# Decay rows of the SSD scan at 128 contraction rows, y products in another order, down weights in 8 KB runs

## The chip, the cores and the metric

One NeuronCore of one Trainium2 chip runs the whole kernel. The metric is the device time in microseconds (us) of one execution. Three executions of the kernel before are shown; their median is what a change is held against. A second, profiled execution gives every duration below.

## The reference, cut to what matters

A decoder block over 512 tokens of width 1024: RMSNorm with adaptive shift and scale, a Mamba-2 SSD branch beside a pooling branch, an output projection, then a mixture of 32 experts of which each token takes 4, and a final norm. The change touches two places. In the SSD branch, for each chunk of 128 tokens and each head:

```python
a_cum = jnp.cumsum(a, axis=-1)
seg = a_cum[..., :, None] - a_cum[..., None, :]
decay = jnp.exp(jnp.where(causal, seg, -jnp.inf))
CB = jnp.einsum('bclgn,bcsgn->bcgls', Cc, Bc)
y_diag = jnp.einsum('bcgls,bcgels,bcsgep->bclgep', CB, decay, X)
...
y_off = jnp.einsum('bclgn,bcgepn,bcgel->bclgep', Cc, prev, jnp.exp(a_cum))
return (y_diag + y_off).reshape(b, s, SSD_HEADS, P)
```

There are 4 chunks, 4 groups, 8 heads of width 64 in a group. In the experts, for the tokens that chose expert e:

```python
gu = xblk @ w_gu[e] + b_gu[e]
...
return act @ w_down[e] + b_down[e]
```

## The kernel before, in words

All work is written in one program for five engines. TensorE (PE) multiplies, VectorE (DVE) and ScalarE (ACT) work elementwise, GpSimd (POOL) and SyncE (SP) mostly issue transfers. A scheduler in the framework decides, before the run, in which order each engine takes its instructions; on the chip each engine then follows its own list strictly and waits on semaphores.

**Projections.** A product of float32 exactness is made of three products of rounded operands: every loaded weight piece is split into a rounded part and a rest (ACT line 117, DVE line 118), and PE multiplies high by high, high by low and low by high. In `proj` these are lines 265, 266 and 267; in `ssd_out` lines 653 to 655; in the experts lines 1118 to 1120. Each is one matmul of 128 contraction rows, 128 output rows and 512 columns. The experts that got few tokens (the "half" ones) skip the split and multiply float32 directly (line 1113).

**SSD.** The program calls `ssd(g)` for the groups g = 0 to 3, with the projections of group g + 1 written behind it (`proj_bc`, `proj_z`, `proj_xs`), then `ssd_out(g)`. The scheduler interleaves these, so that PE takes projection matmuls while ACT and DVE prepare operands. Group 3 is interleaved with gate projections. In `ssd(g)`, four head pairs `hp` follow one another. For each head of a pair:

- the decay row: a matmul copies the head's row of the cumulated decay `AH` to all partitions (line 601). `AH` is a tile of 64 rows, high parts in rows 0 to 31 and rests in rows 32 to 63, and `E` picks the head;
- ACT forms 4 pieces of the decay (line 604), `exp` of 384 columns for the chunk states (line 606) and `exp` of 512 columns for the inner part (line 607);
- DVE multiplies the two results by the `CB` and `C` products (helper at line 114): `dec` and `eC`.

Then the y products of the pair: 8 matmuls of `Xd` with `dec` (line 617) and 6 of the chunk states `Hs` with `eC` (line 619; the first chunk has no state). Each gives 64 output rows and 128 columns; the head h2 of the pair writes rows 0 to 63 or 64 to 127 of the bank `py`. A float32 matmul stands in the trace as two instructions, so a pair of heads has 28.

```python
for c in range(NB):
    cc = slice(c * P, (c + 1) * P)
    hs = [slice(hp * P + h2 * 64, hp * P + h2 * 64 + 64) for h2 in range(2)]
    for h2 in range(2):
        TE.matmul(py[h2 * 64:(h2 + 1) * 64, cc], c3(Xd)[:, c, hs[h2]], decs[h2][:, cc], start=True, stop=c == 0)
    for h2 in range(2 if c else 0):
        TE.matmul(py[h2 * 64:(h2 + 1) * 64, cc], Hs[c][:, hs[h2]], eCs[h2][:, (c - 1) * P:c * P], start=False, stop=True)
```

So a pair needs three shapes of the PE array: 64 rows by 128 columns (line 601), 128 by 64 (lines 617 and 619) and 128 by 128 (everything else around it).

**Experts.** `fetch` (line 771) loads 1 MB pieces from SP's queue into a ring of buffers: 8 pieces of `wgu` and 4 of `wdn` for each of the 32 experts. A `wgu` piece is 128 rows of 8 KB, one for each partition. A `wdn` piece is 256 rows of 4 KB, two for each partition, which lie 128 rows apart in memory.

Of the kernel before, what the change touches and what calls it, by code (L numbers as in the profile page):

```python
# [10 lines left out]
F32R = mybir.dt.float32r  # L11
BF16 = mybir.dt.bfloat16
I32 = mybir.dt.int32
U32 = mybir.dt.uint32
AF = mybir.ActivationFunctionType
# [5 lines left out]
P = 128  # L21
D = 1024
T = 512
NB = 4
KD = 8
NH = 32
NE = 32
# [41 lines left out]
def hybrid_block(ctx: ExitStack, tc: tile.TileContext, cst, cols, rows, xt, xf, wad0, wada, bada,  # L69
                 wx, wz, wdt, wu, wg, wso, wpl, wpo, wo, wr, ball, wgu, wdn, out):  # L70
    nc = tc.nc
    V, S, G, TE, SP = nc.vector, nc.scalar, nc.gpsimd, nc.tensor, nc.sync
# [9 lines left out]
    def T_(tag, cols_, dt=F32, parts=P):  # L82
        if tag in shared:
            o = shared[tag]
            return Z[0:parts, o:o + cols_]
        uid[0] += 1
        return sb.tile([parts, cols_], dt, tag=tag, name=f"{tag}_{uid[0]}")
# [104 lines left out]
    E = T_("E", 32, F32R)  # L192
# [131 lines left out]

    dt, negA, a2 = T_("dt", P), T_("negA", NH), T_("a2", 2 * P)
    ac, dte, eac, cdk = T_("ac", P), T_("dte", P), T_("eac", P), T_("cdk", P)
    AH = T_("q7", 512, F32R, parts=64)

    def make_dt():
        w = load(wdt, n=256)  # L330
        ps = bank("mm")
        for k in range(KD):
            j = k % 4 * 32
            TE.matmul(ps[j:j + 32, :], w[:, k * NH:(k + 1) * NH], xk(k), start=k < 4, stop=k >= 4)
        dfm = T_("q8", 512)
        S.activation(dfm, ps, AF.Copy)
        pdt = bank("ss")
        for b in range(NB):
            TE.transpose(pdt[:, b * P:(b + 1) * P], dfm[:, b * P:(b + 1) * P], ident)

        dx, da, dq, dp = T_("q9", P), T_("q10", P), T_("q11", P), T_("t1", P)
        V.tensor_reduce(v3(dx), pdt.rearrange("p (b j h) -> p b h j", b=NB, j=4), axis=AX.X, op=ALU.add)
        tt(v3(dx), v3(dx), rowb(R_DB), ALU.add)
        V.tensor_scalar(da, dx, -1.0, None, op0=ALU.mult)
        tt(da, da, dx, ALU.max)
        S.activation(da, da, AF.Exp, scale=-1.0)
        V.tensor_scalar(dq, da, 2.0, None, op0=ALU.add)
        V.reciprocal(dq, dq)
        tt(da, da, dq, ALU.mult)
        tt(dq, da, da, ALU.mult)  # L350
        V.tensor_scalar(dp, dq, 2.0 / 19.0, None, op0=ALU.mult)
        for n in (17, 15, 13, 11, 9, 7, 5, 3):
            stt(dp, dp, 2.0 / n, dq, ALU.add, ALU.mult)
        stt(dp, dp, 2.0, da, ALU.add, ALU.mult)
        stt(dt, dx, 0.0, dp, ALU.max, ALU.add)
        S.activation(negA, rw[:, R_AL:R_AL + NH], AF.Exp)
        V.tensor_scalar(negA, negA, -1.0, None, op0=ALU.mult)
        a2v = a2.rearrange("p (c r h) -> p c r h", c=NB, r=2)
        for r in range(2):
            tt(a2v[:, :, r, :], v3(dt), negA.unsqueeze(1).to_broadcast([P, NB, NH]), ALU.mult)  # L360
        pa = bank("ss")
        TE.matmul(pa[:, 0:P], tri, a2v[:, :, 0, :], start=True, stop=True)
        TE.matmul(pa[:, P:2 * P], ones, a2v[:, :, 0, :], start=True, stop=True)
        V.tensor_copy(ac, pa[:, 0:P])
        tt(dte, pa[:, P:2 * P], ac, ALU.subtract)
        S.activation(dte, dte, AF.Exp)
        S.activation(eac, pa[:, 0:P], AF.Exp)
        S.activation(cdk, pa[:, P:2 * P], AF.Exp)
        pah = bank("ss")
        for c in range(NB):  # L370
            TE.matmul(pah[0:64, c * P:(c + 1) * P], a2[:, c * 64:(c + 1) * 64], tri, start=True, stop=True)
        S.activation(AH, pah[0:64, :], AF.Copy)
        V.tensor_tensor(AH[32:64, :], pah[32:64, :], AH[32:64, :].bitcast(F32), op=ALU.subtract)


# [137 lines left out]
    def c3(ap):  # L513
        return ap.rearrange("p (c l) -> p c l", c=NB)
# [66 lines left out]
    def ssd(g):  # L581
        (Cf, Bt, CB), (Xd, y), z = bcs[g], xys[g], zs[g]
        Hs = [None]
        for c in range(NB - 1):
            xw = xw_rot()
            tt(h3(xw), h3(c3(Xd)[:, c, :]), hb(dte, 8 * g, 8, c), ALU.mult)
            pst = bank("ss")
            TE.matmul(pst, Bt[:, c * P:(c + 1) * P], xw, start=True, stop=True)
            H = H_rot()
            if c == 0:  # L590
                S.activation(H, pst, AF.Copy)
            else:
                tt(h3(H), h3(Hs[c]), hb(cdk, 8 * g, 8, c), ALU.mult)
                tt(H, H, pst, ALU.add)
            Hs.append(H)
        for hp in range(4):
            decs, eCs = [], []
            for h2 in range(2):
                hg = 8 * g + hp * 2 + h2
                pseg = bank("ss")  # L600
                TE.matmul(pseg, E[0:64, hg:hg + 1].to_broadcast([64, P]), AH, start=True, stop=True)
                dec, eC = dec_rot(), eac_rot()[:, 0:384]
                for c in range(NB):
                    S.activation(dec[:, c * P:(c + 1) * P], pseg[:, c * P:(c + 1) * P], AF.Relu, scale=-1.0,
                                 bias=ac[:, c * NH + hg:c * NH + hg + 1])
                S.activation(eC, pseg[:, P:512], AF.Exp)
                S.activation(dec, dec, AF.Exp, scale=-1.0)
                tt(dec, dec, CB, ALU.mult)
                tt(eC, eC, Cf[:, P:512], ALU.mult)
                decs.append(dec)  # L610
                eCs.append(eC)
            py = bank("ss")
            for c in range(NB):
                cc = slice(c * P, (c + 1) * P)
                hs = [slice(hp * P + h2 * 64, hp * P + h2 * 64 + 64) for h2 in range(2)]
                for h2 in range(2):
                    TE.matmul(py[h2 * 64:(h2 + 1) * 64, cc], c3(Xd)[:, c, hs[h2]], decs[h2][:, cc], start=True, stop=c == 0)
                for h2 in range(2 if c else 0):
                    TE.matmul(py[h2 * 64:(h2 + 1) * 64, cc], Hs[c][:, hs[h2]], eCs[h2][:, (c - 1) * P:c * P], start=False, stop=True)
            fs = slice(hp * 512, (hp + 1) * 512)  # L620
            f = 4 * g + hp
            stt(y[:, fs], y[:, fs], qc[:, Q_DS + f:Q_DS + f + 1], py, ALU.mult, ALU.add)
            tt(y[:, fs], y[:, fs], z[:, fs], ALU.mult)
            S.activation(z[:, fs], y[:, fs], AF.Square)
            if hp:
                tt(z[:, 0:512], z[:, 0:512], z[:, fs], ALU.add)
        pss = bank("ss")
        for c in range(NB):
            TE.matmul(pss[:, c:c + 1], z[:, c * P:(c + 1) * P], ones[:, 0:1], start=True, stop=True)
        ss4 = T_("ss4", 4)  # L630
        S.activation(ss4, pss[:, 0:4], AF.Sqrt, bias=eps4, scale=1.0 / 512.0)
        V.reciprocal(ss4, ss4)
        prs = bank("ss")
        for c in range(NB):
            TE.matmul(prs[:, c * P:(c + 1) * P], ss4[:, c:c + 1].to_broadcast([P, P]), ident, start=True, stop=True)
        yh, yl = T_("S7", 2048, F32R), T_("S8", 2048, F32R)
        for i in range(4):
            fs = slice(i * 512, (i + 1) * 512)
            stt(y[:, fs], y[:, fs], qc[:, Q_SN + 4 * g + i:Q_SN + 4 * g + i + 1], prs, ALU.mult, ALU.mult)
            split(yh[:, fs], yl[:, fs], y[:, fs])  # L640
        yhl[g] = (yh, yl)
# [101 lines left out]
    def weights(e):  # L743
        def of(w, lo_, hi_):
            return w[e, lo_:hi_, :] if isinstance(e, int) else w[bass.ds(e, 1), lo_:hi_, :].squeeze(0)

        return dict(wu=lambda k: of(wgu, k * P, (k + 1) * P), got={},
                    wd=lambda c: of(wdn, c * 256, (c + 1) * 256).rearrange("(k p) d -> p k d", p=P))

    order = order_of_ranks()  # L750
    big = order.index(NE - 1)
# [13 lines left out]
    def fetch(w, kind, k, t=None):  # L765
        if t is None:
            t = ring.pop(0)
            if t not in ("S7", "r3", "S3"):
                ring.append(t)
        r = T_(t, 2048)  # L770
        SP.dma_start(r if kind == "wu" else r.rearrange("p (k d) -> p k d", k=2), w[kind](k))
        return r

    def eload(w, kind, k):
# [582 lines left out]
    prev, parts, pend, begin = None, [], [], []  # L1357
    for u in range(NE + 1):
        hooks = {}
        if u < NE:  # L1360
            w, sel = weights_of(u), sel_of(u)
# [73 lines left out]
    with tc.For_i(0, nov, 1) as i:  # L1435
        lastp.clear()
        w = tabled(bass.ds(i, 1))
# [45 lines left out]
def _layout(i):  # L1483
    A = np.ascontiguousarray
# [7 lines left out]
    def halves(w):  # L1492
# [19 lines left out]
        wu=A(pairs(tiles(w_in[:, 5152:6176]))),  # L1512
# [4 lines left out]
        wo=A(halves(i["w_out"][0]).reshape(4, P, 2048)),  # L1517
        wr=A(i["w_router"][0].reshape(KD, P, NE).transpose(1, 0, 2).reshape(P, 256)),
        ball=A(np.concatenate([i["b_gu"][0], i["b_down"][0]], axis=1).reshape(NE, 3, 2, 512).transpose(2, 0, 1, 3).reshape(2, NE, 1536)),
        wgu=A(i["w_gu"][0]), wdn=A(i["w_down"][0]))  # L1520
    return d


# [17 lines left out]
```

## Time and profile before

| what | value |
|---|---|
| median of 3 runs | 1842.26 us |
| the 3 runs | 1841.16, 1842.26, 1846.85 us |
| profiled execution: its time | 1837.33 us |
| profiled execution: its span | 1835.5 us |
| PE busy | 1754.0 us, 96% of the span |
| DVE busy | 1210.0 us, 66% |
| ACT busy | 947.1 us, 52% |
| mean rate of transfers | 288 GB/s, about 400 in most of the second half |

The span runs from the first to the last instruction of the profiled execution; 1.8 us of its time lie around it. A busy PE is not one at its peak: matmuls overlap, so the distance from one start to the next tells the pace, and the duration of a single one does not. The SSD groups lie between 211 and 543 us, the experts between about 700 us and the end.

### The profile page before, as it was taken

How to read it: one execution, taken by the hardware profiler on the slowest of the kernel's cores; microseconds unless marked ns; L12 is line 12 of the kernel's file. 1: busy time of each engine (PE TensorE's matmuls, PEld its weight loads, DVE VectorE, ACT ScalarE, POOL GpSimd, SP SyncE). 2: the span in 40 equal slices, each digit the busy share in tenths (PEclk: the TensorE clock that was granted, in tenths of full speed). 3: DMA queues.
4: the chain of work that ended last, by engine and by line, in shares of the span. 5: the costliest groups of instructions: out<-in, count | busy, mean ns of one | idle time of the engine just before them, and what ended most of it. 6: DMA issues, size and time to landing. Idle time of an engine off the chain costs nothing. (4 is left out here: it accounts for less than half of the span.)

```text
span 1835.5 us, 23325 instructions
## 1 busy us (share of the span) xinstructions
PE 1754.0 (96%) x8352; PEld 1161.8 (63%) x8353; DVE 1210.0 (66%) x1803; ACT 947.1 (52%) x1458; POOL 237.5 (13%) x214
## 2 busy tenths in 40 slices
PE   6999999999999999999999999999999999999995
PEld 3777687777778877455566465455564565677741
DVE  5888685858564558666576565375675585799933
ACT  4533554537362346355455455264555465677833
POOL 0000001010000002112111111121212112212111
PEclk8999999999999999999999999999999999999998
DMA  9265334253444368899999999789999999999894
GB/s 355 75 241 218 115 115 138 83 137 103 116 115 183 127 226 321 324 403 396 413 402 394 407 404 352 289 331 374 396 402 394 402 402 365 405 360 342 313 370 192
DMA packets 102728, 527.81 MB, mean 288 GB/s; under 512 B 11737, under 2 KB 12377, under 8 KB 60368
## 3 DMA queue, kind: packets, MB, share of 16 engines
q1 hardware_dynamic: 90544, 498.14, 69.7%
q0 software_dynamic: 11184, 25.50, 6.4%
q10 hardware_dynamic: 880, 2.64, 0.4%
q8 instruction: 67, 1.10, 0.2%
q14 instruction: 53, 0.43, 0.1%
HBM read 502.89 MB, written 25.77 MB: 288 GB/s over the span
## 5 line engine op out<-in xcount | busy, mean ns | idle before, releaser
L118 DVE TENSOR_TENSOR wl<-r,wh 128x1024 fp32r<-128x1024 f32 x246 | 301.3, 1252 | 105.0 <-ACT wh L117 87.0
L117 ACT ACTIVATE wh<-r 128x1024 fp32r<-128x1024 f32 x246 | 254.0, 1057 | 133.0 <-PE mm L266 56.3
L118 DVE TENSOR_TENSOR wl<-S,wh 128x1024 fp32r<-128x1024 f32 x186 | 229.3, 1268 | 32.8 <-ACT wh L117 32.2
L1119 PE MATMUL mm<-wl,S 128*128 128x512 f32 x540 | 214.2, 397 | 8.0 <-DVE wl L118 7.7
L117 ACT ACTIVATE wh<-S 128x1024 fp32r<-128x1024 f32 x186 | 190.0, 1056 | 54.0 <-PE mm L1120 30.2
L1120 PE MATMUL mm<-wh,S 128*128 128x512 f32 x540 | 213.0, 394 | 0.0
L265 PE MATMUL mm<-S,wh 128*128 128x512 f32 x512 | 206.5, 404 | 3.9 <-ACT S L117 3.9
L267 PE MATMUL mm<-S,wl 128*128 128x512 f32 x512 | 205.1, 401 | 1.5 <-DVE wl L118 1.5
L266 PE MATMUL mm<-S,wh 128*128 128x512 f32 x512 | 205.5, 401 | 0.0
L1118 PE MATMUL mm<-wh,S 128*128 128x512 f32 x540 | 182.1, 400 | 1.9 <-ACT wh L117 1.4
L1154 DVE TENSOR_SCALAR q<-mm 128x512 f32<-128x512 f32 x49 | 33.5, 688 | 151.9 <-PE mm L1113 124.6
L1155 ACT ACTIVATE q<-q 128x512 f32<-128x512 f32 x50 | 31.5, 632 | 192.2 <-DVE q L1154 192.0
L1118 PEld LDWEIGHTS mm<-wh,S 128*128 128x128 f32 x540 | 101.1, 188 | 39.3 <-issue 9.7
L1119 PEld LDWEIGHTS mm<-wl,S 128*128 128x128 f32 x540 | 101.3, 188 | 37.2 <-DVE wl L118 14.2
L265 PEld LDWEIGHTS mm<-S,wh 128*128 128x128 f32 x512 | 96.4, 188 | 32.8 <-issue 6.8
L1120 PEld LDWEIGHTS mm<-wh,S 128*128 128x128 f32 x540 | 101.4, 188 | 21.8
L267 PEld LDWEIGHTS mm<-S,wl 128*128 128x128 f32 x512 | 96.3, 188 | 29.5 <-issue 6.6
L266 PEld LDWEIGHTS mm<-S,wh 128*128 128x128 f32 x512 | 96.5, 188 | 26.6 <-issue 4.2
L1119 PE MATMUL ss<-wl,S 128*128 128x512 f32 x240 | 98.8, 412 | 3.1 <-DVE wl L118 3.1
L1120 PE MATMUL ss<-wh,S 128*128 128x512 f32 x240 | 94.8, 395 | 0.0
L1113 PE MATMUL mm<-S,S 128*64 128x512 f32 x408 | 94.5, 595 | 0.0
L1179 POOL TENSOR_TENSOR y<-y,q 128x512 f32<-128x512 f32 x47 | 63.7, 1367 | 209.7 <-ACT y L1178 209.7
(498 smaller groups left out, 3086.9 us busy)
## 6 DMA issues: line engine op xcount, KB each, us to landing
S<-in_wgu SPq DMA_DIRECT2D x113, 1024.0 KB, 12.1
r<-in_wgu SPq DMA_DIRECT2D x97, 1024.0 KB, 10.1
S<-in_wdn SPq DMA_DIRECT2D x61, 1024.0 KB, 12.7
r<-in_wdn SPq DMA_DIRECT2D x44, 1024.0 KB, 14.9
bc<-in_wgu SPq DMA_DIRECT2D x23, 1024.0 KB, 11.3
Z<-in_wgu SPq DMA_DIRECT2D x23, 1024.0 KB, 10.1
r<-in_wada SPq DMA_DIRECT2D x16, 1024.0 KB, 6.0
r<-in_wx SPq DMA_DIRECT2D x12, 1024.0 KB, 6.2
```

Source lines behind the costliest of these rows:

```text
L117: S.activation(hi, src, AF.Copy)
L118: V.tensor_tensor(lo, src, hi.bitcast(F32), op=ALU.subtract)
L265: TE.matmul(ps, a, hh(k), start=k == 0, stop=False)
L266: TE.matmul(ps, a, hl(k), start=False, stop=False)
L267: TE.matmul(ps, b, hh(k), start=False, stop=k == KD - 1)
L1113: lastp[:] = [TE.matmul(rows_of(ps, n0 + i), x.c[k], hl[:, o + i * 512:o + (i + 1) * 512], start=False, stop=stop).ins]
L1118: TE.matmul(p, x.h[k], h, start=False, stop=False)
L1119: TE.matmul(p, x.h[k], l, start=False, stop=False)
L1120: lastp[:] = [TE.matmul(p, x.l[k], h, start=False, stop=stop).ins]
L1154: V.tensor_scalar(g, pg, LIM, None, op0=ALU.min)
L1155: S.activation(t, g, AF.Tanh, scale=ALPHA / 2)
L1179: G.tensor_tensor(yn, yn, gaf2[0] if half else gaf[n], op=ALU.mult)
```

## The change

`AH` becomes a tile of 128 rows, whose rows 64 to 127 are set to zero once by POOL, and the decay-row matmul takes all 128 rows of `E` and `AH`. `E` repeats its 32 columns' pattern in every 32 rows, so rows 64 to 127 of `E` are not zero, those of `AH` are. The y products go through the chunks in the order 1, 2, 3, 0, in each first the chunk states (the second head ahead of the first), then the inner part. The host lays `w_down` out so that the two 4 KB rows of a partition lie side by side.

```diff
-    AH = T_("q7", 512, F32R, parts=64)
+    AH = T_("q7", 512, F32R)
+    G.memset(AH[64:P, :].bitcast(U32), 0)
...
-        S.activation(AH, pah[0:64, :], AF.Copy)
+        S.activation(AH[0:64, :], pah[0:64, :], AF.Copy)
...
-                TE.matmul(pseg, E[0:64, hg:hg + 1].to_broadcast([64, P]), AH, start=True, stop=True)
+                TE.matmul(pseg, E[:, hg:hg + 1].to_broadcast([P, P]), AH, start=True, stop=True)
...
-            for c in range(NB):
+            for c in (1, 2, 3, 0):
                 cc = slice(c * P, (c + 1) * P)
-                hs = [slice(hp * P + h2 * 64, hp * P + h2 * 64 + 64) for h2 in range(2)]
-                for h2 in range(2):
-                    TE.matmul(py[h2 * 64:(h2 + 1) * 64, cc], c3(Xd)[:, c, hs[h2]], decs[h2][:, cc], start=True, stop=c == 0)
-                for h2 in range(2 if c else 0):
-                    TE.matmul(py[h2 * 64:(h2 + 1) * 64, cc], Hs[c][:, hs[h2]], eCs[h2][:, (c - 1) * P:c * P], start=False, stop=True)
+                hs = [slice(hp * P + h2 * 64, hp * P + h2 * 64 + 64) for h2 in (1, 0)]
+                for h2, h in zip((1, 0) if c else (), hs):
+                    TE.matmul(py[h2 * 64:(h2 + 1) * 64, cc], Hs[c][:, h], eCs[h2][:, (c - 1) * P:c * P], start=True, stop=False)
+                for h2, h in zip((1, 0), hs):
+                    TE.matmul(py[h2 * 64:(h2 + 1) * 64, cc], c3(Xd)[:, c, h], decs[h2][:, cc], start=c == 0, stop=True)
...
-                    wd=lambda c: of(wdn, c * 256, (c + 1) * 256).rearrange("(k p) d -> p k d", p=P))
+                    wd=lambda c: of(wdn, c * P, (c + 1) * P))
...
-        SP.dma_start(r if kind == "wu" else r.rearrange("p (k d) -> p k d", k=2), w[kind](k))
+        SP.dma_start(r, w[kind](k))
...
-        wgu=A(i["w_gu"][0]), wdn=A(i["w_down"][0]))
+        wgu=A(i["w_gu"][0]), wdn=A(i["w_down"][0].reshape(NE, 4, 2, P, D).transpose(0, 1, 3, 2, 4)).reshape(NE, 4 * P, 2 * D))
```

From line 328 on every line of the changed kernel stands one further down, so that the decay row is line 602 there, and of the y products the chunk states are line 618 and the inner part is line 620.

The scheduler puts the new program into another order on PE. In the first group of the kernel before, behind two projection matmuls, PE takes one y product of the first pair (bank `ss_1561`), then the decay rows of the second pair (`ss_1579`, `ss_1590`), four projection matmuls and the other 13:

```order
L266 MATMUL mm_1741<-S_39_155,wh_265_1735 128x512
L267 MATMUL mm_1741<-S_37_153,wl_266_1736 128x512
L617 MATMUL ss_1561<-q_235_1540,S_190_1187 64x128
L601 MATMUL ss_1579<-q_66_386,E_118 128x512
L601 MATMUL ss_1590<-q_66_386,E_118 128x512
L265 MATMUL mm_1741<-S_37_153,wh_265_1735 128x512
L266 MATMUL mm_1741<-S_39_155,wh_265_1735 128x512
L267 MATMUL mm_1741<-S_37_153,wl_266_1736 128x512
L265 MATMUL mm_1741<-S_37_153,wh_265_1735 128x512
L617 MATMUL ss_1561<-q_237_1551,S_190_1187 64x128
L617 MATMUL ss_1561<-q_235_1540,S_190_1187 64x128
```

The same place in the changed kernel (bank `ss_1562`, decay rows `ss_1580` and `ss_1591`):

```order
L266 MATMUL mm_1742<-S_39_155,wh_265_1736 128x512
L267 MATMUL mm_1742<-S_37_153,wl_266_1737 128x512
L265 MATMUL mm_1742<-S_37_153,wh_265_1736 128x512
L618 MATMUL ss_1562<-q_238_1553,q_227_1523 64x128
L618 MATMUL ss_1562<-Z,q_227_1523 64x128
L602 MATMUL ss_1580<-q_66_386,E_118 128x512
L602 MATMUL ss_1591<-q_66_386,E_118 128x512
L620 MATMUL ss_1562<-q_237_1552,S_190_1188 64x128
L620 MATMUL ss_1562<-q_235_1541,S_190_1188 64x128
L618 MATMUL ss_1562<-q_238_1553,q_230_1529 64x128
```

The y products of the pair now start later in PE's list, behind 17 projection matmuls where there were 13, and run to their end with nothing but the next pair's two decay rows between them.

Behind that run, the kernel before alternates between single instructions, with y products of the second pair (`ss_1602`) and the decay rows of the third (`ss_1621`, `ss_1632`) among the projections:

```order
L619 MATMUL ss_1561<-q_238_1552,q_233_1535 64x128
L266 MATMUL mm_1741<-S_39_155,wh_265_1735 128x512
L617 MATMUL ss_1602<-q_241_1581,S_190_1187 64x128
L267 MATMUL mm_1741<-S_37_153,wl_266_1736 128x512
L601 MATMUL ss_1621<-q_66_386,E_118 128x512
L265 MATMUL mm_1772<-S_36_152,wh_265_1735 128x512
L601 MATMUL ss_1632<-q_66_386,E_118 128x512
L266 MATMUL mm_1772<-S_38_154,wh_265_1735 128x512
```

In the changed kernel 17 projection matmuls follow one another there, then all 14 y products of the second pair (`ss_1603`), then the third pair's decay rows:

```order
L620 MATMUL ss_1562<-q_235_1541,S_190_1188 64x128
L266 MATMUL mm_1742<-S_39_155,wh_265_1736 128x512
L267 MATMUL mm_1742<-S_37_153,wl_266_1737 128x512
L265 MATMUL mm_1773<-S_36_152,wh_265_1736 128x512
L266 MATMUL mm_1773<-S_38_154,wh_265_1736 128x512
L267 MATMUL mm_1773<-S_36_152,wl_266_1737 128x512
L265 MATMUL mm_1773<-S_36_152,wh_265_1736 128x512
```

The whole first group reads, with F for a full-array matmul, R for a decay row, P for a y product and the number of neighbours behind each letter: before R2 F13 P1 R2 F4 P13 F1 P1 F1 R1 F1 R1 F8 P13 F9 P1 R2 F4 P4 F3 P9 F1 P1 F15 P13, now R2 F17 P2 R2 P12 F17 P14 R2 F20 P2 R2 P12 F20 P14. The other groups follow the same pattern; in the last one the third stretch has 32 full-array matmuls and the last pair's y products are parted 2 and 12 by two of them.

On SP, between the last SSD group and the last `ssd_out`, loads change places with reads of the summed-up SSD output `ys_d`. Before:

```order
L724 DMA q_580_4361<-mod_d 128x512
L715 DMA S_564_4223<-ys_d 128x512 x3
L155 DMA r_566_4225<-in_wso 128x2048
L715 DMA S_564_4223<-ys_d 128x512
L724 DMA q_581_4362<-mod_d 128x512
L155 DMA r_586_4369<-in_wg 128x2048
L771 DMA Z_4903<-in_wdn 128x2x1024
L715 DMA S_565_4224<-ys_d 128x512 x3
L155 DMA r_573_4293<-in_wso 128x2048
```

Now:

```order
L155 DMA r_586_4370<-in_wg 128x2048
L155 DMA r_566_4226<-in_wso 128x2048
L772 DMA Z_4904<-in_wdn 128x2048
L716 DMA S_564_4224<-ys_d 128x512 x4
L155 DMA r_573_4294<-in_wso 128x2048
L725 DMA q_580_4362<-mod_d 128x512
L725 DMA q_581_4363<-mod_d 128x512
L716 DMA S_565_4225<-ys_d 128x512 x4
```

The first weights of `ssd_out` and of the gates now stand ahead of the reads of `ys_d`. In the experts no engine's list changes, but for the shape of the `wdn` pieces.

## Rows read from the trace of the kernel before

**Rows 1.** The page: busy time of the engines; DMA share in 40 slices.

```profile
PE 1754.0 (96%) x8352; PEld 1161.8 (63%) x8353; DVE 1210.0 (66%) x1803; ACT 947.1 (52%) x1458; POOL 237.5 (13%) x214
...
DMA  9265334253444368899999999789999999999894
```

**Rows 2.** Waits of SP's queue, 780 to 1120 us: total, times, longest (us).

```profile
SPq L771 <- DVE wl L118: 106.4, 47, 5.5
```

**Rows 3.** Waits of PE in the same stretch: total, times, longest (us).

```profile
PE ss L1066 <- DVE q L111: 7.7, 5, 1.6
```

**Rows 4.** Timeline of PE, a stretch of projections: start, duration (us), instructions, count.

```profile
238.97 0.50 PE L267 MATMUL mm<-S,wl 128*128 128x512 f32 x1
239.31 0.40 PE L265 MATMUL mm<-S,wh 128*128 128x512 f32 x1
...
243.26 0.39 PE L267 MATMUL mm<-S,wl 128*128 128x512 f32 x1
```

**Rows 5.** Timeline of PE, single decay rows among projections.

```profile
220.64 0.49 PE L601 MATMUL ss<-q,E 64*128 64x512 f32 x1
221.07 0.51 PE L265 MATMUL mm<-S,wh 128*128 128x512 f32 x1
221.50 0.49 PE L601 MATMUL ss<-q,E 64*128 64x512 f32 x1
221.92 0.50 PE L266 MATMUL mm<-S,wh 128*128 128x512 f32 x1
222.25 0.40 PE L267 MATMUL mm<-S,wl 128*128 128x512 f32 x1
```

**Rows 6.** Timeline of PE, one y product and two decay rows.

```profile
215.28 0.39 PE L267 MATMUL mm<-S,wl 128*128 128x512 f32 x1
215.60 0.43 PE L617 MATMUL ss<-q,S 128*64 128x128 f32 x2
215.96 0.72 PE L601 MATMUL ss<-q,E 64*128 64x512 f32 x2
216.62 0.50 PE L265 MATMUL mm<-S,wh 128*128 128x512 f32 x1
216.95 0.40 PE L266 MATMUL mm<-S,wh 128*128 128x512 f32 x1
```

**Rows 7.** Timeline of PE, a run of 13 y products, its first and last neighbours.

```profile
223.98 0.54 PE L617 MATMUL ss<-q,S 128*64 128x128 f32 x5
...
225.65 0.50 PE L265 MATMUL mm<-S,wh 128*128 128x512 f32 x1
226.00 0.39 PE L266 MATMUL mm<-S,wh 128*128 128x512 f32 x1
```

**Rows 8.** Timeline of PE, the first decay rows of group 0.

```profile
211.72 0.73 PE L601 MATMUL ss<-q,E 64*128 64x512 f32 x2
```

**Rows 9.** Timeline of ACT and DVE behind them (in brackets the idle time before).

```profile
212.25 1.15 ACT L604 ACTIVATE q<-ss,Z 128x128 f32<-128x128 f32 x4 [1.74 <-PE ss L601]
...
215.15 0.55 ACT L606 ACTIVATE q<-ss 128x384 f32<-128x384 f32 x1
...
215.73 1.21 DVE L114 TENSOR_TENSOR q<-q,bc 128x384 f32<-128x384 f32 x2 [0.72 <-ACT q L606]
```

**Rows 10.** Timeline of ACT: a convolution's first step, and a weight split.

```profile
222.91 0.83 ACT L506 ACTIVATE r<-mm,Z 128x512 f32<-128x512 f32 x1
...
412.60 1.07 ACT L117 ACTIVATE wh<-r 128x1024 fp32r<-128x1024 f32 x1
```

**Rows 11.** Timeline of PE and of ACT ahead of group 2.

```profile
414.27 1.12 PE L588 MATMUL ss<-q,bc 128*128 128x512 f32 x2 [1.96 <-DVE q L114]
...
410.21 0.60 ACT L661 ACTIVATE y<-mm 128x512 f32<-128x512 f32 x1 [6.23 <-DMA ys_d<-y]
```

**Rows 12.** DMA issues: count, size, median us from issue to landing.

```profile
Z<-in_wgu SPq DMA_DIRECT2D x23, 1024.0 KB, 10.1
...
Z<-in_wdn SPq DMA_DIRECT2D x11, 1024.0 KB, 10.5
```

## The prediction, made before the changed kernel ran

> **What bounds the kernel now.** I read the page first: PE is busy 96% of the span, no other engine over 66% [rows 1]. That alone says little, since overlapped matmuls all count as busy, so I read PE's timeline and measured from start to start. Where projections follow one another the pace is (243.26 - 239.31) / 17 = 0.232 us for a matmul of 512 columns [rows 4]; I write 0.233. In the SSD groups that pace breaks wherever the array's shape changes, and those breaks are what the change is about.
>
> Then the experts, because over half of the time and the third edit lie there. Transfers look full there: the DMA digits are 8 or 9 in all but two slices from the 16th on [rows 1]. But who waits decides. Between 780 and 1120 us SP's queue waits above all for DVE to finish with a buffer (106.4 us in 47 waits) [rows 2], while the largest item of PE's own waits is 7.7 us in five, for DVE [rows 3]; the other two kinds of wait that PE has there are shorter and for DVE as well. So PE sets the pace of the experts, the ring of buffers holds the transfers back, and whatever PE saves in the SSD groups moves everything behind it forward.
>
> **The prices of a change of shape**, all in us from start to start.
> - Single decay rows (64 by 128) and single projections in turn: 220.64, 221.07, 221.50, 221.92, so 0.43 each instead of 0.233 [rows 5].
> - Two decay rows together: 215.96 to 216.62 = 0.66, instead of 0.466 [rows 6].
> - The first full-array matmul behind a change: 216.62 to 216.95 = 0.33 [rows 6] or 225.65 to 226.00 = 0.35 [rows 7], which is 0.10 over the pace. The last one ahead of a change: 215.28 to 215.60 = 0.32, 0.09 over [rows 6]. A stretch between two changes so costs 0.19.
> - One y product alone: 215.60 to 215.96 = 0.36 [rows 6]. Thirteen in one run: 223.98 to 225.65 = 1.67 [rows 7]. The two heads of a chunk write different halves of the columns and run side by side, so 13 take as long as 14: seven pairs. I split 1.67 into 0.15 for leaving and 7 x 0.217.
>
> Check on group 0 as it is: y products 4 x 0.36 + 3 x 1.67 + (0.58 + 1.24 for the runs of 4 and 9) = 8.27; decay rows 3 x 0.66 + 2 x 0.43 = 2.84; projections 4 single ones x 0.43 + 56 x 0.233 + 0.09 + 6 x 0.19 = 16.00. Sum 27.11. Measured from the first decay row [rows 8] to the projection behind the last y product [rows 4]: 238.97 - 211.72 = 27.25. The prices hold.
>
> **The change part by part.**
> 1. *Decay rows at 128 rows, and y products in whole runs.* Work at pace in group 0 before: 60 projections and 8 decay rows x 0.233 + 28 pairs x 0.217 = 21.9, so 27.25 holds 5.3 of breaks. The new list has 74 projections; decay rows are now full-array matmuls and need no change of shape. Runs: twice P2 (0.37), P12 (1.45) and P14 (1.67) = 6.98; 82 full-array matmuls x 0.233 = 19.11; edges 0.09 + 5 x 0.19 = 1.04. Sum 27.1, of which 82 x 0.233 + 6.08 = 25.2 is work, so 1.9 are breaks. Group 0 gives back 3.4. Priced from their lists in the same way, the breaks of groups 1 to 3 before are 5.0, 5.0 and 5.5; after 1.9 each. In all 20.8 - 7.6 = **13.2 us** less on PE.
>    Changes of shape within the groups' stretch go from some 100 to some 50, so a change costs about a quarter of a us with all that hangs on it.
>    The unknown is the pace of a decay row of 128 rows, which no row shows. From below it can't beat 0.233 (the pace of the same shape [rows 4]); from above 0.33 each (the pair of 64 rows [rows 6]), which would cost 32 x 0.10 = 3.2. I take 0.233, since its shape is that of the projections, whose weight loads are hidden.
>    Here a rule of the Trainium skill speaks against the edit. Rows 4 show a 128-row matmul every 0.232 us, each with its own weights. "TensorE: Matmul & The Clock Gate" (What overlaps and what doesn't) says that a weight load overlaps a running matmul only when its row group differs; by it no load could hide among full-height matmuls, padding would gain nothing, and the sum would be some 3 us smaller. Rows 4 speak against it.
> 2. *Waits that the new order adds.* The first y product of a pair now needs the second head's `eC`, the last thing ready, and the next pair's decay rows stand behind it on PE. In group 0 ACT begins 0.53 behind the first decay row (212.25), starts the second head's `exp` at 215.15, and DVE's multiplication of it starts at 215.73 [rows 9]; of the two that take 1.21 the first has 384 of 896 columns, so it ends near 216.3, 4.6 behind the decay row. PE comes there after 19 matmuls: 19 x 0.233 + 0.09 = 4.5. So PE waits 0.1 to 0.2 in the first pair of each group. The third pair has 20 projections ahead (5.4 us); its chain is longer, since ACT first squares the pair before; I count it as just covered. The second and fourth pair have the rest of a run and 17 or 20 projections, some 6 us: covered. I charge 0.6 for all; the range has 0 to 8 (a us in each of eight places).
> 3. *The zeroing on POOL* is one instruction at the program's start, where POOL has nothing else and the first reader comes after 200 us: 0. Without that cover it would be about the time of a copy of that size on another engine, under 1 us.
> 4. *SP's list behind the last group.* Weights go ahead of the reads of `ys_d`. Between the last y product and `ssd_out` lie 20 + 9 + 67 full-array matmuls, 22 us; hidden, 0. One missed read would cost a few us: the longest such wait on `ys_d`, for its accumulating writes, held ACT 6.2 [rows 11].
> 5. *Down weights in 8 KB runs.* A piece lands in 10.5 us, an up piece (8 KB runs already) in 10.1 into the same buffers [rows 12]. PE waits for neither [rows 3], and the queue waits for buffers [rows 2]: 0. From above: had transfers set the pace of all 128 down pieces (2.6 us each at 400 GB/s, 333 us), 0.4 / 10.5 of that, 12.7. From below nothing is lost, since the new form is that of the up pieces.
>
> Sum: 13.2 - 0.6 = 12.6 us less. Against the profiled execution 1837.33 - 12.6 = 1824.7. That execution lies 4.9 under the median of the runs, so against the median **1842.26 - 12.6 = 1829.7**.
>
> **The rivals.**
> - *Given back behind the groups.* PE comes earlier to `ssd_out`, whose results leave through two buffers and accumulating transfers. ACT already stood 6.23 us for one of them, and PE stood 1.96 ahead of group 2 [rows 11]. If that chain sets the pace of groups 1 and 2, the 3.1 us of each come back as waits: 12.6 - 6.2 = 6.4 less, 1835.9. Against it: PE's stretch of `ssd_out` is unchanged, so the transfers start earlier by as much as PE does.
> - *The padded decay row keeps its price* (the bound of part 1): 9.4 less, 1832.9.
> - *Transfers set the pace somewhere after all*, most likely in the runs that are slower than the profiled one: up to 12.7 more, 1817; a third of it is likelier, 1825.
> - *The breaks are not of shape.* The lists before put an instruction alone just where its operand came ready, so 0.43 could be a wait for a semaphore, which a new order keeps. Then 0 to 3 less, about 1841. Against it: the projections at 221.07 and 221.92 need nothing new and take 0.43 as well [rows 5].
> - *Slower.* PE's list is strict, and eight places now have the next decay rows behind a y product that needs the end of ACT's and DVE's chain. If ACT has a convolution's step (0.83) and both halves of a weight split (2 x 1.07) [rows 10] in front of the exps there, PE stands 2.97 each time: 8 x 2.97 = 23.8, 11.2 slower than now, 1853.5. The gain is gone from 1.6 a place. Against it: ACT's new list has only the squares and a convolution's step or two between the pairs.
>
> **How the numbers follow.** About 0.3%, 5.5 us, is what a measurement of this kernel can tell from no change. Forecast (10 to 14 less) 0.66; given back 0.12; the padded price 0.05; transfers 0.08; not of shape 0.05; slower 0.04. Faster by over 0.3%: forecast, padded price, transfers and half of what is given back, 0.85. Within: the other half, not of shape, and a part of the slower case, 0.12. Slower 0.03. The range runs from 1821 (the forecast with half of what transfers could add) to 1837 (all given back, or 8 us of waits at the y products); it leaves out the last two rivals and the far end of the third.
>
> **What would show it.** Right: in PE's timeline 128-row decay rows 0.233 apart and y products in runs of 14; group 0 from its first decay row to the end of its 74th projection's run in some 27.1 us though it holds 14 projections more; the end of the last group's y products no later than before; the experts' stretch as long as before, starting 12 to 13 us sooner. Wrong: PE waits for DVE's multiplications (line 114) of over a us ahead of y products, a longer wait at line 588, or a shorter period of the experts, which would mean that transfers did count.

## The result, and the profile after

| | kernel before | changed kernel |
|---|---|---|
| median of 4 runs each | 1842.77 us | **1826.51 us** |
| lowest and highest | 1841.16, 1846.85 us | 1824.71, 1828.25 us |
| profiled execution: time, span | 1837.33, 1835.5 us | 1824.71, 1822.9 us |

The ratio is **0.9915, with a 95% interval of 0.9892 to 0.9938**: faster by 16.3 us between the medians and by 12.6 us between the profiled executions. Predicted were 1829.7 us, and 12.6 us less for the profiled execution.

PE's list around the first pairs of group 0 [rows 5 to 8]. Timeline of PE in the changed kernel; columns are start, duration (both us), engine, line, operation, out<-in, array shape, count:

```profile
210.04 1.04 PE L602 MATMUL ss<-q,E 128*128 128x512 f32 x2
210.92 0.39 PE L267 MATMUL mm<-S,wl 128*128 128x512 f32 x1
...
214.65 0.39 PE L265 MATMUL mm<-S,wh 128*128 128x512 f32 x1
214.99 0.32 PE L618 MATMUL ss<-q,q 128*64 128x128 f32 x1
...
215.36 0.72 PE L602 MATMUL ss<-q,E 128*128 128x512 f32 x2
216.01 0.44 PE L620 MATMUL ss<-q,S 128*64 128x128 f32 x4
...
217.47 0.50 PE L266 MATMUL mm<-S,wh 128*128 128x512 f32 x1
...
221.31 0.39 PE L267 MATMUL mm<-S,wl 128*128 128x512 f32 x1
221.63 0.32 PE L618 MATMUL ss<-q,q 128*64 128x128 f32 x1
...
223.31 0.72 PE L602 MATMUL ss<-q,E 128*128 128x512 f32 x2
223.87 0.39 PE L265 MATMUL mm<-S,wh 128*128 128x512 f32 x1
```

Three things are to be seen. The first y product starts at 214.99, right behind the projection at 214.65 (0.34, where a change of shape alone took 0.32 [rows 6]): where part 2 of the prediction put a wait there is none over 0.02. The 17 projections between the first and the second pair run from 217.47 to 221.31 at (221.31 - 217.81) / 15 = 0.233, counted from the second of them on, where the kernel before alternated between single instructions. And a run of 14 y products takes 223.31 - 221.63 = 1.68.

Where the time went is read from the starts of the same instruction in both traces (us):

| place on PE | before | after | shift |
|---|---|---|---|
| line 210, its third place, near the start | 40.45 | 39.29 | -1.17 |
| line 588, first of group 0 | 208.75 | 207.57 | -1.18 |
| line 653, first of `ssd_out(0)` | 284.32 | 279.73 | -4.59 |
| line 588, first of group 1 | 307.26 | 302.61 | -4.66 |
| line 588, first of group 2 | 408.56 | 400.80 | -7.75 |
| line 588, first of group 3 | 510.05 | 499.06 | -10.99 |
| line 588, last of group 3 | 514.33 | 505.68 | -8.65 |
| line 653, first of `ssd_out(3)` | 574.81 | 562.78 | -12.04 |
| line 1113, first (experts begin) | 737.60 | 725.36 | -12.24 |
| line 1205, last (experts end) | 1815.43 | 1803.14 | -12.29 |

The four groups give back 3.4, 3.1, 3.2 and 3.4, together 13.1. Two entries have nothing to do with the breaks. At the start 1.2 us are gained at once: the window of 20 to 40 us shows a granted clock of 0.80 before and 0.91 after, and from 40 us to the end of the experts both are at 1.00. And ahead of group 3, 2.3 us are lost again. The experts' stretch is as long as it was: 1815.43 - 737.60 = 1077.83 before, 1077.78 after.

Its waits read as before [rows 2, 3], though a down piece takes half as many packets (all packets of the kernel: 102728 before, 86344 after). Waits of SP's queue and of PE, 780 to 1120 us, changed kernel (total, times, longest), and the issues of the pieces [rows 12]:

```profile
SPq L772 <- DVE wl L118: 115.4, 49, 6.2
```

```profile
PE ss L1067 <- DVE q L111: 7.8, 5, 1.6
```

```profile
Z<-in_wgu SPq DMA_DIRECT2D x23, 1024.0 KB, 9.5
Z<-in_wdn SPq DMA_DIRECT2D x11, 1024.0 KB, 10.0
```

PE stalls twice at line 589 (588 before), the product of the chunk states that comes just ahead of a group's first decay rows: 1.94 ahead of group 2, where the kernel before stood 1.96 [rows 11], and 2.34 ahead of group 3, where it did not stand in its profile. Waits of PE, 200 to 560 us, changed kernel:

```profile
PE ss L589 <- DVE q L114: 4.3, 2, 2.3
```

Ahead of group 3, the timelines of PE, of DVE and of ACT (in brackets the idle time before the instruction and what ended it):

```profile
502.41 0.40 PE L266 MATMUL mm<-S,wh 128*128 128x512 f32 x1
505.14 1.12 PE L589 MATMUL ss<-q,r 128*128 128x512 f32 x2 [2.34 <-DVE q L114]
```

```profile
502.66 1.23 DVE L118 TENSOR_TENSOR wl<-r,wh 128x1024 fp32r<-128x1024 f32 x1 [11.04 <-ACT wh L117]
...
504.41 0.68 DVE L114 TENSOR_TENSOR q<-S,Z 128x512 f32<-128x512 f32 x1
```

```profile
494.43 0.60 ACT L662 ACTIVATE y<-mm 128x512 f32<-128x512 f32 x1 [1.57 <-DMA ys_d<-y]
501.08 0.60 ACT L662 ACTIVATE y<-mm 128x512 f32<-128x512 f32 x1 [6.05 <-DMA ys_d<-y]
501.57 1.05 ACT L117 ACTIVATE wh<-r 128x1024 fp32r<-128x1024 f32 x1
```

Read from the end: PE waits for DVE's weighting of a chunk at line 114; DVE stood 11.04 in its strict list for ACT's rounded weights at line 117; ACT stood 6.05 in its own for a staging buffer of `ssd_out`, held by an accumulating transfer to `ys_d`. This chain is the one that the prediction's first rival named, and a longer wait at line 588 was one of its signs of being wrong. The second profiles below show that the longer wait is not the change's.

### The profile page after: what moved, and what is told of

It is laid out like the page before. It is cut to its first block, busy times and chain, and to the rows that moved or that the text cites. A ratio compares the mean times of both kernels' runs of the same rounds, so it can differ in the third digit from the quotient of the medians.

```text
span 1822.9 us, 23331 instructions
## 1 busy us (share of the span) xinstructions
PE 1739.8 (95%) x8353; PEld 1160.5 (64%) x8353; DVE 1211.0 (66%) x1803; ACT 947.8 (52%) x1458; POOL 238.7 (13%) x215
## 2 busy tenths in 40 slices
DMA packets 86344, 527.81 MB, mean 290 GB/s; under 512 B 11737, under 2 KB 12377, under 8 KB 27600
```

## The experiments

Each kernel was timed against the kernel before on the same chip. Between those sets the median of the kernel before was 1842.77, 1839.46, 1842.42 and 1840.89 us, so only kernels of one set are subtracted from each other.

**The parts, one at a time** (kernel before 1839.46).

*The decay rows alone*, on the kernel before:

```diff
-                TE.matmul(pseg, E[0:64, hg:hg + 1].to_broadcast([64, P]), AH, start=True, stop=True)
+                TE.matmul(pseg, E[:, hg:hg + 1].to_broadcast([P, P]), AH, start=True, stop=True)
```

with the 128-row `AH` and its zeroing.

> Only the decay rows are changed (128 contraction rows over zero rows); y products and down weights as before. Theory (each change of the array's shape has a price): the y products keep 34 runs on TensorE, but the decay rows no longer break the stream; priced from this kernel's list, the breaks of the four SSD groups fall from 21.3 to 15.3 us, so 6 us less than before, and each decay row takes 0.233 us from start to start. Rival (a weight load hides only beside another row group): the decay rows keep 0.33 to 0.43 us, 0 to 3 us less. Rival (the breaks are waits for operands): no change.

1832.83 us, ratio 0.9963 (0.9950 to 0.9975), 6.6 less. PE's order is that of before, so the place of [rows 5] can be laid beside it. Timeline of PE:

```profile
219.51 0.50 PE L267 MATMUL mm<-S,wl 128*128 128x512 f32 x1
219.85 0.40 PE L602 MATMUL ss<-q,E 128*128 128x512 f32 x1
220.08 0.40 PE L265 MATMUL mm<-S,wh 128*128 128x512 f32 x1
220.31 0.39 PE L602 MATMUL ss<-q,E 128*128 128x512 f32 x1
220.54 0.39 PE L266 MATMUL mm<-S,wh 128*128 128x512 f32 x1
```

The same instructions in the same order, waiting for the same semaphores, now go at 0.23 instead of 0.43. Only the rows of the decay matmul changed, so the breaks are of shape, and a padded decay row has the price of a projection.

The weight loads of the same matmuls (PEld) show what a break is made of. First the kernel before, then the decay rows alone:

```profile
221.92 0.19 PEld L266 LDWEIGHTS mm<-S,wh 128*128 128x128 f32 x1 [0.24 <-issue]
222.03 0.19 PEld L267 LDWEIGHTS mm<-S,wl 128*128 128x128 f32 x1
```

```profile
220.08 0.19 PEld L602 LDWEIGHTS ss<-q,E 128*128 128x128 f32 x1
220.32 0.19 PEld L266 LDWEIGHTS mm<-S,wh 128*128 128x128 f32 x1
```

Behind the change of shape the load of line 266 starts together with its own matmul at 221.92 [rows 5]; that of line 267, of the same shape as its neighbour, starts at 222.03, 0.22 ahead of its matmul at 222.25. With the padded rows each load starts with the matmul ahead of its own (220.08 for the one at 220.31). A load of 0.18 to 0.19 that no longer runs beside the matmul ahead, on top of 0.233, makes 0.42, which is close to the 0.43 seen. That is read from starts; no run separates the load from anything else that a change of shape may bring.

*The order of the y products alone*, on the kernel before:

```diff
-            for c in range(NB):
+            for c in (1, 2, 3, 0):
```

with the chunk states first, as in the change; the decay rows keep 64 rows.

> Only the order of the y products is changed; decay rows stay at 64 rows, down weights in 4 KB runs. Theory: the y products go in 24 runs instead of 34 and the decay rows stand in pairs; priced from this kernel's list, breaks fall from 21.3 to 10.4 us, so about 11 us less than before, and less still by 2 to 3 us if the wait ahead of group 3 comes here too. Rival (breaks are waits): no change, or slower by the later start of each pair's y products.

1829.51 us, ratio 0.9944 (0.9926 to 0.9963), 10.0 less.

*The down weights alone*, on the kernel before:

```diff
-                    wd=lambda c: of(wdn, c * 256, (c + 1) * 256).rearrange("(k p) d -> p k d", p=P))
+                    wd=lambda c: of(wdn, c * P, (c + 1) * P))
```

> Only the down weights are changed, to 8 KB runs. Theory (TensorE sets the pace of the experts, transfers wait for buffers): no change, within 1 us; the pairs of experts keep their period of 66.1 us. Rival (in the runs without a profile transfers set the pace now and then): 3 to 5 us less, which would be the part of the 16.3 us between the medians that the profiles' difference of 12.6 us does not hold.

1841.76 us, ratio 1.0011 (0.9993 to 1.0029): no change clear of the scatter, though the median lies 2.3 higher where 1 was allowed. The experts of its profile last 1077.78, those of the kernel before 1077.83.

*The change without the down weights* (that edit undone, the other two kept):

> The whole change but for the down weights, which stay in 4 KB runs. Theory: the same as the whole change in its profile, 12 to 13 us less than before. Rival (transfers): 3 to 5 us slower than the whole change in the medians.

1824.54 us, ratio 0.9920 (0.9901 to 0.9939), 14.9 less. The 8 KB runs bring nothing that can be measured, alone or with the rest.

The two edits that count share what they save. By the starts of line 588 (589), from the first of group 0 to the first of group 2, a stretch without waits of PE: the decay rows alone save 3.25 - 0.12 = 3.13 us, the order alone 5.45 (from +1.05 to -4.40), both together 7.75 - 1.18 = 6.57, and 6.56 without the down weights. In the new order half of the decay rows stand between y products, where they are a change of shape on either side with 64 rows or with 128. So the sum of the two is 2 us too much over these two groups.

**The stall at line 589** (kernel before 1842.42; the changed kernel again, 1826.99).

*Four staging buffers instead of two*, in groups 1 and 2, on the changed kernel. The two new ones are buffers that are free there. The order on PE, DVE and SP stays; on ACT a convolution's step (line 511) goes ahead of one copy, although the expectation had every order unchanged:

```diff
+    def st_four():
+        st_n[0] += 1
+        return T_("q6" if st_n[0] % 4 == 1 else "q16", 512) if st_n[0] % 2 else st_rot()
...
-            st = st_rot()
+            st = st_four() if g else st_rot()
```

> The changed kernel, but the results of ssd_out in groups 1 and 2 are staged in four buffers (the two halves of y and two more) instead of two, so that ScalarE's copy waits for the transfer four back. Every engine's order stays. Theory (the waits ahead of groups 2 and 3 come from the accumulating transfers that hold ScalarE): ScalarE's waits for these transfers fall from 29 us to under 15, the waits of 1.94 and 2.34 us ahead of the two groups at line 589 go, and the kernel comes out 3 to 5 us faster than the changed kernel timed beside it, some 1821. Rival (the transfers themselves set the pace of these stretches, however many buffers): the waits stay over 1.5 us each, the time stays within 1.5 us. Rival (ScalarE's other work is what is late): the waits at line 589 stay although ScalarE no longer stands.

**1822.17 us, ratio 0.9887 (0.9866 to 0.9909)**, 4.8 less than the changed kernel beside it. In groups 1 and 2 no wait of ACT for `ys_d` is left, where the changed kernel had 22.3 in six (group 0, which keeps two buffers, still has two, 6.4 together), and from 200 to 560 us PE has no wait over 0.3. Timelines of PE and of ACT at the place shown above (lines stand 6 further down):

```profile
500.76 0.40 PE L266 MATMUL mm<-S,wh 128*128 128x512 f32 x1
500.99 1.08 PE L595 MATMUL ss<-q,r 128*128 128x512 f32 x2
```

```profile
494.87 0.60 ACT L668 ACTIVATE q<-mm 128x512 f32<-128x512 f32 x1 [2.18 <-PE mm L662]
497.38 1.06 ACT L117 ACTIVATE wh<-r 128x1024 fp32r<-128x1024 f32 x1 [1.91 <-PE mm L661]
```

ACT now waits for PE instead of a transfer, and its split at line 117 starts ahead of PE's need.

*One staging buffer instead of two*:

```diff
-            st = st_rot()
+            st = st_rot.t[:, 0:512] if g else st_rot()
```

> The changed kernel, but with one staging buffer in groups 1 and 2 instead of two. This doubles the suspected wait. Theory (a buffer is held for 4.5 to 8 us by its accumulating transfer, and ScalarE's strict list stands for it): ScalarE stands before nearly each of the 16 copies, 60 to 110 us in all instead of 29, its weight splits and the chain to line 589 come late, and TensorE loses 20 to 80 us. Rival (the buffers do not matter): under 5 us slower.

1847.89 us, ratio 1.0032 (1.0015 to 1.0049), 20.9 more than the changed kernel. Waits of ACT and of PE, 200 to 560 us:

```profile
ACT y L662 <- DMA ys_d<-y: 61.6, 16, 6.3
...
PE ss L589 <- DVE q L114: 18.9, 2, 9.6
```

Of these 16 waits two belong to group 0, whose buffers stay; in groups 1 and 2, 14 of 16 copies stand 55.1 where it was 22.3, and the two stalls at line 589 grow from 4.3 to 18.9. With two buffers more the stall goes, with one less it grows fourfold; the rivals of both runs fall.

*The changed kernel again*, for its scatter:

> The changed kernel itself, beside the others. By its parts timed alone: 1824 to 1827, ratio 0.991 to 0.993. Theory on its own scatter (a wait ahead of groups 2 and 3 differs from run to run, and the granted clock falls to its lower level for some us behind the longer ones): this profile shows waits there of another length than 1.94 and 2.34 us, and a stretch of granted clock 0.50 only behind waits that are longer than about 2.3 us. Rival: the same two waits to 0.1 us.

1826.99 us (1824.24 to 1829.71), ratio 0.9919 (0.9897 to 0.9940). Its profile shows 1.54 and 0.56 where the first showed 1.94 and 2.34: the stall has another length in each execution.

What the length follows can be read from the traces. Ahead of group 2, ACT stands for the accumulating transfer issued fifth there (at 401.27 in the kernel before, at 393.51 in the changed one, so 7.76 earlier, as PE's own work is). Its time from issue to landing and PE's stall, in all nine profiles with two buffers (us):

| y products | profile | transfer | stall of PE | difference |
|---|---|---|---|---|
| order of before | kernel before | 8.84 | 1.96 | 6.88 |
| | kernel before, once more | 10.15 | 3.27 | 6.88 |
| | down weights alone | 9.84 | 2.98 | 6.86 |
| | decay rows alone | 9.25 | 2.38 | 6.87 |
| new order | changed kernel | 8.81 | 1.94 | 6.87 |
| | changed kernel again | 8.41 | 1.54 | 6.87 |
| | without the down weights | 8.04 | 1.17 | 6.87 |
| | down weights in 2 KB runs | 10.30 | 3.42 | 6.88 |
| | order of the y products alone | 9.42 | 2.54 | 6.88 |

The stall is the transfer's time less 6.87, whichever way PE's list is ordered. Ahead of group 3 it is less exact: transfers of 7.57 to 8.65 go with stalls of 2.02 to 2.97, those of 5.12 to 5.60 with none to 0.85 (kernel before: 5.18 and none, once more 7.57 and 2.02). Why the same transfer takes longer in one execution than in another was not tried.

*Down weights in 2 KB runs*, on the changed kernel:

```diff
-                    wd=lambda c: of(wdn, c * P, (c + 1) * P))
+                    wd=lambda c: of(wdn, c * 512, (c + 1) * 512).rearrange("(k p) d -> p k d", p=P))
```

> The changed kernel, but the down weights lie in runs of 2 KB, a quarter of the length in the changed kernel and half of that before; the bytes are the same. Theory (the ring's buffers hold the transfers back, not the chip's rate): within 2 us of the changed kernel timed beside it; a down piece takes longer from issue to landing than 10.1 us, and SP's queue waits less for buffers. Rival (short runs cost, and 8 KB against 4 KB gained what was too small to see): 3 us or more slower.

1825.86 us, ratio 0.9907 (0.9885 to 0.9930), 1.1 less than the changed kernel beside it, which is within the scatter of both. The page and the waits of SP's queue, 780 to 1120 us:

```profile
DMA packets 135496, 527.81 MB, mean 289 GB/s; under 512 B 11737, under 2 KB 12377, under 8 KB 93136
```

```profile
SPq L772 <- DVE wl L118: 103.1, 42, 8.9
```

There are 49152 packets more and the queue still stands for buffers, somewhat less than the 115.4 above. The time from issue to landing, which was expected to grow, is not given in this trace.

**Why the medians moved by more than the sum** (kernel before 1840.89).

*The kernel before with four staging buffers* (the edit above, nothing else):

> The kernel before with nothing changed but the four staging buffers in groups 1 and 2; TensorE's order stays. Question: the change gave about 3 us more between the medians than between the two profiled executions. Theory (the waits ahead of groups 2 and 3 and the fall of the granted clock behind them, whose length scatters, make up that part): no wait over 0.5 us at line 588 ahead of the groups, no granted clock below 0.95 between 200 and 560 us, 3 to 7 us less than the kernel before, and a spread of the runs under 7 us where the kernel before had 10. The four-buffer version of the changed kernel then lies 12 to 14 us below this one, which is the price of the breaks alone (13.2). Rival (the scatter comes from elsewhere, the start or the experts): under 2 us less, and the same spread.

1836.30 us, ratio 0.9969 (0.9957 to 0.9982), 4.6 less, and 12 runs lie within 3.2 us (1834.02 to 1837.24) where 17 of the kernel before lie within 10.7 (1836.56 to 1847.24). No stall ahead of a group, no fall of the clock from 200 to 560 us.

*The changed kernel with four staging buffers, again*:

> The four-buffer version of the changed kernel again, for its distance to the same version of the kernel before: 12 to 14 us less than that by the breaks alone. If the change had a second effect outside the breaks and these waits, the distance would be 15 us or more; if part of the breaks were waits at semaphores, 10 or less.

1823.08 us, ratio 0.9895 (0.9874 to 0.9915). The distance to the run above is 1836.30 - 1823.08 = **13.2 us**, the breaks alone. Their traces agree: from the first product of group 0 to the first of the experts PE takes 526.53 and 513.00, 13.5 less.

*The kernel before, once more*:

> The kernel before, unchanged, for one more profile of it. Theory: its waits at line 588 ahead of groups 2 and 3 have other lengths than 1.96 and 0.4 us, and where one is over about 2.3 us the granted clock is 0.50 for some us behind it. Rival: the same lengths to 0.1 us.

1842.08 us, 4.75 over the first profiled execution of the same kernel. Its stalls are 3.27 and 2.02. Behind the longer one the pace halves; timeline of PE, then windows of 5 us (the last three numbers are the granted clock, the DMA share and GB/s):

```profile
414.63 1.13 PE L588 MATMUL ss<-q,bc 128*128 128x512 f32 x2 [3.27 <-DVE q L114]
...
417.43 0.63 PE L265 MATMUL mm<-S,wh 128*128 128x512 f32 x1
417.85 0.63 PE L266 MATMUL mm<-S,wh 128*128 128x512 f32 x1
418.28 0.63 PE L267 MATMUL mm<-S,wl 128*128 128x512 f32 x1
```

```profile
405.00:410.00 5.00, 5.00 (x19) 3.39 (x18) 0.00 (x0) 0.00 (x0) 0.00 (x0) 1.00 0.80 195
...
415.00:420.00 5.00, 5.00 (x12) 2.99 (x11) 3.81 (x6) 3.48 (x12) 0.00 (x0) 0.57 0.87 221
420.00:425.00 5.00, 5.00 (x19) 3.01 (x19) 1.21 (x2) 2.00 (x6) 0.00 (x0) 0.75 0.09 39
```

Projections stand 0.43 apart instead of 0.233, the engine's lower level of 1.2 GHz for 2.4. From ahead of this stall to the first matmul of `ssd_out(2)` this execution falls 4.3 us behind the first one (shift -0.94 to +3.38): 3.27 - 1.96 = 1.3 is the longer stall, the other 3.0 the clock behind it. Group 3 adds 2.0, its stall. Together 6.4 lost behind a start that was 0.94 earlier, so 5.4 at the end of the groups and 5.46 at the end of the experts.

## Why the prediction was right, point by point

- **Part 1, the breaks: right.** 13.2 us were summed from the lists and six prices; the groups gave 3.4, 3.1, 3.2 and 3.4 in the trace (predicted 3.4, 3.1, 3.1 and 3.6), and the pair of kernels without the scattering stall differs by 13.2. The details hold as well: 14 y products in 1.68 (1.67 was taken), a pair of decay rows between y products in 216.01 - 215.36 = 0.65 (0.466 + 0.19 was taken). Group 0 was to take 27.1 from its first decay row and took 27.6, from 210.04 to the projection at 237.63; but this decay row now starts 0.03 behind the last product of line 589 (210.01) and runs beside it, where before it started 0.53 behind (211.19, 211.72). From the projection behind the two decay rows it is 237.63 - 210.92 = 26.7, against 27.1 - 2 x 0.233 - 0.09 = 26.5.
- **The padded decay row: right.** 0.23 was taken, from bounds of 0.233 and 0.33; the decay rows alone show 0.23. The rule of the Trainium skill that spoke against it ("TensorE: Matmul & The Clock Gate", What overlaps and what doesn't) doesn't agree with this trace: each of these matmuls takes all 128 rows and its own weights, and the loads still hide.
- **Part 2, the new waits: wrong.** 0.6 was charged ahead of the first y products, and none over 0.02 came in the first pair. It was close: DVE's first product for the second head ends at 214.93, 4.9 behind the first decay row where 4.6 was taken, and PE came 4.95 behind it where 4.5 was counted, since that row now starts beside the product ahead of it. So the place was well chosen, but the term should have been nothing.
- **The first rival, given back behind the groups, falls.** In this pair of profiles it looks as if it had come true at a third of its price, 2.34 ahead of group 3 where the kernel before had none. But the kernel before, once more, stands 2.02 there and the changed kernel again 0.56; ahead of group 2 the stall is the transfer's time less 6.87 with either list. So the prediction's argument against it held: the transfers start earlier by as much as PE does. The medians of the kernels with two buffers differ by 16.3 and 15.4, not by less than the 13.2 of those with four. What the prediction did not have is that the stall's length follows a transfer whose time differs from execution to execution.
- **That the profiles differ by just 12.6 is partly luck.** 13.1 from the groups and 1.2 from an earlier rise of the clock at the start, less 2.3 for the stall, make 12.0; small gains up to the experts (0.2) and from there to the end of the span (0.3) make up the rest. The 1.2 are not the change's: the decay rows alone had 1.1 at line 210 and were down to 0.1 at line 540 (157 us), and the unchanged kernel itself started 0.94 earlier in its second profile.
- **Against the median, 3.2 too high.** The step at fault is that the sum was carried over to a median of three runs. Medians of the kernel before scatter by 3.3 us between sets, because its stalls ahead of groups 2 and 3 and the clock behind them scatter; with four buffers its runs lie within 3.2 (what is left is taken up in the last section). All runs shown here together give 1840.64 (61 runs) against 1826.60 (10 runs), a difference of 14.0.
- **Parts 3 to 5: right.** The zeroing takes 0.52 us at 0.72 us, long before its reader. Nothing is seen of SP's new list, or of the 8 KB runs. For the last, the experiments go from 2 to 8 KB and find nothing: buffers hold these transfers back, as rows 2 and 3 said.
- **The other rivals fall.** The breaks are of shape (the decay rows alone), transfers do not set the pace (down weights alone), no y product waits for DVE.
- **Two slips in the sums, without consequence.** The check of group 0 counts seven stretches of projections but six leading edges; with the seventh, 0.10, it gives 27.2, nearer to the 27.25 measured. And the forecast less half of what transfers could add is 1829.7 - 6.35 = 1823.4, not the 1821 at which the range begins; the result lies inside either.

## What to carry to other kernels

Where matmuls of several shapes alternate at the pace of the array, count the changes of shape from the list and price each from starts, not durations: here about a quarter of a us each (some 54 changes of shape fewer for 13.2 us), and giving a small matmul the shape of its neighbours by zero rows, or putting the odd ones in one run, each saves its breaks, but not the same one twice. Before a profiled gain is carried over to a median, look for stalls whose length changes from run to run; here two more staging buffers in front of an accumulating transfer took 4.8 us from the changed kernel and two thirds of the scatter from the kernel before. A full queue of transfers is no bound while it waits for buffers: a quarter of the run length changed nothing.

## What the runs showed of the hardware beyond that

A stall of PE can cost more than its length. Ahead of groups 2 and 3, the granted clock fell to its lower level with the stalls of 2.38, 2.42, 2.54, 2.97, 2.98, 3.27 and 3.42 us, and of 9.30 and 9.61 with one buffer, and with none of 0.56 to 2.34. In the case shown above the fall cost 3.0 us, nearly as much as the stall of 3.27 itself. The Trainium skill ("TensorE: Matmul & The Clock Gate", What's actually happening) lists two states of this clock, 1.2 and 2.4 GHz; windows of 1 us inside such a stretch agree. One of them, in the kernel with the order of the y products alone, behind its stall of 2.54:

```profile
413.00:414.00 1.00, 1.00 (x3) 0.40 (x2) 0.52 (x1) 0.72 (x3) 0.00 (x0) 0.50 0.71 115
```

A stall's length does not decide alone, however, and 2.34 against 2.38 is no border to carry elsewhere. In the experts every profile has the same place where PE stands 1.21 or 1.22 for ACT's rounded weights and, within 3 us behind it, 0.22 for ACT and about half a us for DVE. Behind it the clock fell in five profiles (the three with four buffers, the decay rows alone, and the 2 KB runs) and in the other eight it did not. PE there in the changed kernel with four buffers, then in the changed kernel; the window from 1574 to 1576 us of the first has a granted clock of 0.50, that from 1578 to 1580 of the second 1.00:

```profile
1571.04 0.74 PE L1125 MATMUL mm<-wh,S 128*128 128x512 f32 x2 [1.21 <-ACT wh L117]
...
1574.36 0.63 PE L1127 MATMUL mm<-wh,S 128*128 128x512 f32 x1
1574.79 0.63 PE L1126 MATMUL mm<-wl,S 128*128 128x512 f32 x1
```

```profile
1575.35 0.73 PE L1119 MATMUL mm<-wh,S 128*128 128x512 f32 x2 [1.22 <-ACT wh L117]
...
1579.04 0.40 PE L1121 MATMUL mm<-wh,S 128*128 128x512 f32 x1
1579.27 0.39 PE L1120 MATMUL mm<-wl,S 128*128 128x512 f32 x1
```

In four of the five it fell once more some 177 us later. The experts lasted 1077.6 to 1077.9 without such a fall, 1078.8 with one and 1080.5 to 1080.7 with two. The two kernels with four buffers that give the 13.2 us both have two falls in their profiles (1080.55 and 1080.61), so their difference is untouched. The 3 us of scatter that are left with four buffers are of this size; that they are these falls in the runs without a profile is not shown.

The start of the program differs from execution to execution too: from 20 to 40 us the granted clock was 0.80 before, 0.91 in the changed kernel and with the decay rows alone, 0.83 in the next three experiments. What it depends on there was not tried.
